# Embedding ranked over the rotary tables, a third more of expert 0 split ahead of the overflow check, and delta-rule key tiles of one chunk

## Chip, cores and metric

One core of one Trainium2 chip. The metric is the device time of one execution in microseconds, here the median over runs. Engines are called TensorE (PE), VectorE (DVE), ScalarE (ACT), GpSimd (POOL) and SyncE (SP, which issues most DMAs); L and a number is a line of the kernel.

## What is computed

An encoder trunk of two layers over 16 learned tokens and 1024 input tokens of width 1024, in float32. Shortened from the reference:

```python
h = layer_norm(concat([meta, x]), emb_ln_g, emb_ln_b)
cos, sin = rotary(pos)                        # used by the attention's latents
for li in range(2):
    proj = h @ w_in[li]
    y_att  = mla(c_q, c_kv, k_pe, cos, sin, ...)      # latent attention, 4 heads
    y_rwkv = rwkv_bidir(shifted(rw), ...)             # delta rule, 8 heads of 64, forward + backward
    h = layer_norm(a * h + concat([y_att, y_rwkv]) @ w_out[li])
    h = layer_norm(a * h + hier_moe(h))               # 32 experts, top-2 of one group
return h[:, 16:]

# the delta rule, per head and direction
S = S * w_t - (S @ kk_t) b_t' + v_t k_t' ;  y_t = S @ r_t
```

## The kernel before

Each layer runs in stages: input projection, attention, delta rule, output projection with the router, MoE. A scheduler orders most of the program from the code's order, priorities and its own estimate of times; the MoE's main loop stands in a `manual_schedule()` block and keeps the order in which it is written.

**Start (L279 to L291, L391 to L398).** `embed` takes the 16 learned tokens and then eight tiles of 128 tokens: a load `xt` on SP, a sum on ScalarE (L288), the layer norm on VectorE with a power on GpSimd (L223 to L228), a store to `h_rows`, and a transpose into `hT`, whose high and low parts (`hT_hi`, `hT_lo`) feed the input projection (L201 to L203). Ahead of it in the code stand the rotary tables (L240 to L265; tiles `pi`, `pf`, `ki`, `kf`, `trig`) and per-layer parameters (`cp`, `dcp`).

**MoE (`moe_layer`).** The weights of an expert come as three thirds of 1 MB (`raw`). `third` splits each into a high part on ScalarE (`w_hi`, L1217, four pieces) and a low part on VectorE (`w_lo`, L1221, four pieces). Before the main loop two thirds of expert 0 are split, and a branch (L1309) leads to code for tokens over an expert's capacity; the branch isn't taken at run time here. Then gathered tokens are transposed (`turned`), multiplied with the first two thirds (`first`), gated, transposed again (`upright`), and multiplied with the last third (`product`). `portion(e, q)` splits third q of expert e at its place in the loop. A load of weights needs a free `raw` tile, so it waits on SP for the split of an earlier third.

**Delta rule (`rwkv`, L1488 on).** The sequence is 17 chunks of 64, and two directions walk them, so there are 34 chunk steps a layer, in 17 jobs of two steps (one forward, one backward). A job passes four stages: `grams` (L1495) loads key tiles `T` and `BK`, multiplies them (`e`, L1528), masks the result into T and `AA`, scales BK and transposes it into `BT` (`m`, L1547); `blocks` and `levels` invert the triangular blocks (L1597 to L1618); `chain` (L1638) runs the recurrence, reading T at L1659 (`tu`) and L1666 (`y`), BT at L1683 (`st`), AA at L1690 (`y`), with a state tile `ring` that new_ring (L1625 on) fills on SP. The chains go one behind the other; grams run some jobs ahead. The output projection of the attention (`e` at L201 to L203, with stores and loads `a_d`, `ht`, `yraw` on SP) is filled in between.

T, AA and BT belong to a pool pair that alternates every second job (`svs[j % 4 // 2]`, each with two buffers), so the T of a job takes the buffer of the job four before. BK has two buffers of its own:

```python
T = sv[0].tile([128, U, 2, 128], F32, name="T")        # U = 8: both chunks of the job
BK = kb.tile([128, U, 2, 64], F32, name="BK")
BT = sv[1].tile([128, U, 2, 64], F32, name="BT")
```

Of the kernel before, what the change touches and what calls it, by code (L numbers as in the profile page):

```python
# [11 lines left out]
F32 = mybir.dt.float32  # L12
# [158 lines left out]
def hybrid_encoder(ctx: ExitStack, tc: tile.TileContext, I, out):  # L171
# [184 lines left out]
    for li in range(DEPTH):  # L356
# [32 lines left out]
        with pool(tc, name="ip", bufs=1, side="right") as ip, pool(tc, name="ipw", bufs=2, side="right") as wp, \  # L389
# [2 lines left out]
                pool(tc, name="ipp", bufs=2, space=PSUM) as pp, ExitStack() as late:  # L392
            hT = pair(ip, [128, 8, L], "hT")
            if li == 0:
                embed(hT, pp)
            else:
                combine(li - 1, hT, pp)
            wk = late.enter_context(pool(tc, name="ipk", bufs=1))  # L398
# [781 lines left out]
def moe_layer(tc, I, li, last, K, split, mm3, stack, rt, route, h1_rows, y_rows, nt, dram):  # L1180
# [18 lines left out]
    with pool(tc, name="mop", bufs=1, space=PSUM) as pp:  # L1199
# [177 lines left out]
        nb, nbi, known = excess()  # L1377

        with tc.issue_after(route.act.ins), tc.issue_after(route.dve.ins), tc.issue_after(known.ins), tc.issue_after(second.ins):
            ws = {0: [third(raws[0][q]) for q in range(2)]}  # L1380
        overflow(nb, nbi)


# [24 lines left out]
        with tc.manual_schedule():  # L1408
            xTs[0] = turned(xs[0], CAP)
            first(0, 0)  # L1410
            tokens(2)
            first(0, 1)
            tanh(0)
            gate(0)
            xTs[1] = turned(xs[1], CAP)
            tokens(3)
            portion(0, 2)
            raws.append(of(2))
            aT = upright(ths.pop(0), CAP)
            for q in range(3):  # L1420
                portion(1, q)
            raws.append(of(3))
            for e in range(NE):
                more, new = e + 1 < NE, e + 2 < NE
                if more:
                    first(e + 1, 0)
                portion(e + 2, 0)
                if new:

                    xTs[e + 2] = turned(xs[e % 2], CAP)  # L1430
                    if e + 4 < NE:
                        tokens(e + 4)
                if more:
                    first(e + 1, 1)
                if new:
                    mid, w1 = raws[e + 2][1], pair(ww, [128, 2048], "w")
                    ws[e + 2].append(w1)
                    for c in range(4):
                        high(mid, w1, c)
                        if c < 3:  # L1440
                            low(mid, w1, c)
                if more:
                    tanh(e + 1)
                    gate(e + 1)
                py = product(aT, ws.pop(e)[2], CAP)
                y = wk.tile([128, D], F32, name="y")
                if new:
                    low(mid, w1, 3)
                    raw, w = raws[e + 2][2], pair(ww, [128, 2048], "w")
                    ws[e + 2].append(w)  # L1450
                    for c in range(2):
                        high(raw, w, c)
                        low(raw, w, c)
                scaled(y, py, e, 0)
                if more:
                    aT = upright(ths.pop(e + 1), CAP)
                scaled(y, py, e, 1)
                nc.gpsimd.indirect_dma_start(out=views[e], out_offset=bass.IndirectOffsetOnAxis(ap=VS[:CAP, e:e + 1], axis=0),  # L1458
                                             in_=y[:CAP], in_offset=None, bounds_check=2 * n_rows - 1, oob_is_err=False)
                if new:  # L1460
                    for c in range(2, 4):
                        high(raw, w, c)
                        low(raw, w, c)
                    if e + 4 < NE:
                        raws.append(of(e + 4))


def rwkv(tc, li, last, K, P, pc, kr_d, bk_d, bon_d, g_dram, vt_d, yT, mhalf, kept, side, ready):
# [29 lines left out]
    def grams(runs, sv):  # L1498
# [1 line left out]

        U = 4 * sum(n for _, _, n in runs)

        T = sv[0].tile([128, U, 2, 128], F32, name="T")
        BK = kb.tile([128, U, 2, 64], F32, name="BK")

        at, u0 = [], 0
        for d, c0, n in runs:
            us = slice(u0, u0 + 4 * n)
            at += [(d, c0 + u // 4, u % 4) for u in range(4 * n)]
            u0 += 4 * n  # L1510
            for o, h in enumerate(HALF):
                nc.sync.dma_start(T[h, us, o], kr_d[d, h, c0:c0 + n].rearrange("p c i x -> p (c i) x"))
            cs = bk_d[d, :, c0:c0 + n].rearrange("p c i (a t) -> p (c i) a t", a=2)
            nc.sync.dma_start(BK[lo, us], cs[lo])
            for a in range(2):

                nc.sync.dma_start(BK[hi, us, 1 - a], cs[hi, :, a])
        AA = sv[1].tile([128, U, 128], F32, name="AA")
        A, AR = AA[:, :, :64], AA[:, :, 64:]
        BT = sv[1].tile([128, U, 2, 64], F32, name="BT")  # L1520


        for q0 in range(0, U, 4):
            q = slice(q0, q0 + 4)
            ps = [pe.tile([128, 4, 128], F32, name="e") for _ in HALF]
            for u in range(4):
                for o, h in enumerate(HALF):
                    nc.tensor.matmul(ps[o][:, u], BK[h, q0 + u].rearrange("p a t -> p (a t)"), T[h, q0 + u, o],  # L1528
                                     start=True, stop=True)
            mask = K(f"mask{at[q0][0]}")  # L1530
            for o in range(2):
                a, b = HALF[o], HALF[1 - o]
                V.tensor_tensor(T[b, q, o], ps[o][b], mask[b, None, :].to_broadcast([64, 4, 128]), op=OP.mult)  # L1533
                nc.scalar.activation(AA[a, q], ps[o][a], AF.Copy)  # L1534
        u0 = 0
        for d, c0, n in runs:
# [7 lines left out]
        for q0 in range(0, U, 4):  # L1544
            ps = bank().rearrange("p (a b) -> p a b", a=4)
            for u in range(4):
                nc.tensor.transpose(ps[:, u], BK[:, q0 + u].rearrange("p a t -> p (a t)"), ident)  # L1547
            nc.scalar.activation(BT[:, q0:q0 + 4].rearrange("p u o x -> p u (o x)"), ps, AF.Copy)
        return T, A, AR, BT, {x: u for u, x in enumerate(at)}

    def blocks(As, E):
# [84 lines left out]
    shared = {}  # L1636

    def chain(job, s, Y):  # L1638
        T, _, AR, BT, units = s
        for d, c in job:  # L1640
            ring = rings.pop((d, c))
            x = steps.index((d, c))
            if x + AHEAD < len(steps):
# [12 lines left out]
            tu, ps = shared["tu"][:, x % 2], shared["st"][:, x % 2]  # L1656
            for i in range(4):
                for o in range(2):
                    nc.tensor.matmul(tu[HALF[o], i], T[:, un(i), o, 0:64], ring[:, i, o], start=True, stop=True)  # L1659
            t0 = ch.tile([128, 4, 64], F32, name="t0", bufs=2)  # L1660
            nc.scalar.activation(t0, tu, AF.Copy)
            if want:
                py = pq.tile([128, 4, 64], F32, name="y", bufs=2)
                for i in range(4):
                    for o in range(2):
                        nc.tensor.matmul(py[HALF[o], i], T[:, un(i), o, 64:], ring[:, i, o], start=i == 0, stop=False,  # L1666
                                         skip_group_check=True)
            if more:
                nring = rings[d, orders[d][pos + 1]]
# [10 lines left out]
            if more:  # L1680
                for i in range(4):
                    for o in range(2):
                        nc.tensor.matmul(ps[HALF[o], i], BT[:, un(i), o], ring[:, i, o], start=True, stop=True)  # L1683
                for o in range(2):
                    a = HALF[o]
                    V.tensor_tensor(nring[a, :, o], ps[a], sp[a], op=OP.add)  # L1686
# [108 lines left out]
```

## Time and profile before

| | us |
|---|---|
| median of three runs (lowest, highest) | 3145.37 (3142.09, 3153.57) |
| the profiled execution | 3157.96 |
| its span | 3156.2 |
| TensorE busy in it | 2707.3 (86%) |
| VectorE busy | 2165.3 (69%) |
| ScalarE busy | 1650.5 (52%) |
| GpSimd busy | 1050.7 (33%) |
| mean granted TensorE clock | 0.888 |

The profile is one execution. Busy time of TensorE is the time in which matmuls are under way, at whichever clock was granted; 1.00 is 2.4 GHz and 0.50 is 1.2 GHz. A matmul of the program in plain float32 stands as two records in the trace. Idle time is named after what ended it. The stages lie, in us, at: layer 0 start and input projection 0 to 385, attention to 660, delta rule to 1120, output projection and router to 1200, MoE to 1545; layer 1 the same, with the delta rule at 2250 to 2700 and the MoE at 2760 to 3100.

### The profile page before, as it was taken

What the parts mean: (1) busy time and instruction counts of PE and PEld (TensorE: products, weight loads), DVE (VectorE), ACT (ScalarE), POOL (GpSimd) and SP (SyncE); (2) the same over time, 40 slices, a digit from 0 to 9 for tenths busy, and PEclk for the clock granted to TensorE, in tenths of its full rate; (3) what the DMA queues carried; (4) which work ended last, traced back from release to release, by engine and by line L of the source; (5) the groups of instructions that cost most, each with busy time, mean ns of one, the idle gap of its engine ahead of it and who ended that gap; (6) DMA issues with size and microseconds to landing.
All of it is one profiled execution on the core that took longest, in us unless ns stands there. A gap on an engine that the chain in (4) does not pass through costs nothing. (4 is left out here: it accounts for less than half of the span.)

```text
span 3156.2 us, 58039 instructions
## 1 busy us (share of the span) xinstructions
PE 2707.3 (86%) x22160; PEld 2209.1 (70%) x22160; DVE 2165.3 (69%) x4257; ACT 1650.5 (52%) x3604; POOL 1050.7 (33%) x1049
## 2 busy tenths in 40 slices
PE   5998799979999997999589997988799989799982
PEld 4888688768777775666388866877687777666661
DVE  7568655475766678989756756444667675789896
ACT  5434454444444447888543435434544453488882
POOL 3656211143334532121246631111433353321111
PEclk9999999978887897999789988998788879899996
DMA  5345610233322357999824465201433233699996
GB/s 175 97 137 185 205 48 21 75 93 102 94 68 78 108 198 259 358 360 352 303 91 137 155 194 186 65 21 51 107 108 101 69 93 100 214 333 356 352 347 244
DMA packets 342732, 523.77 MB, mean 166 GB/s; under 512 B 110732, under 2 KB 263308, under 8 KB 315808
## 3 DMA queue, kind: packets, MB, share of 16 engines
q1 hardware_dynamic: 234832, 399.11, 38.8%
q10 hardware_dynamic: 93280, 87.04, 8.1%
q0 software_dynamic: 14336, 33.84, 3.2%
q8 instruction: 176, 2.88, 0.4%
q14 instruction: 108, 0.88, 0.1%
HBM read 406.57 MB, written 129.84 MB: 170 GB/s over the span
## 5 line engine op out<-in xcount | busy, mean ns | idle before, releaser
L1221 DVE TENSOR_TENSOR w_lo<-raw,w_hi 128x512 fp32r<-128x512 f32 x768 | 481.7, 684 | 49.4 <-ACT w_hi L1217 49.1
L1217 ACT ACTIVATE w_hi<-raw 128x512 fp32r<-128x512 f32 x768 | 424.7, 625 | 71.0 <-DMA raw<-in_w_moe_dram 57.3
L201 PE MATMUL pj<-hT_hi,w_hi 128*128 128x352 f32 (+1 forms) x912 | 303.9, 334 | 3.0 <-ACT k L437 2.7
L202 PE MATMUL pj<-hT_lo,w_hi 128*128 128x352 f32 (+1 forms) x912 | 301.8, 331 | 2.8 <-DVE hT_lo L212 2.8
L203 PE MATMUL pj<-hT_hi,w_lo 128*128 128x352 f32 (+1 forms) x912 | 300.3, 330 | 0.0
L201 PE MATMUL ph<-w_hi,xT_hi 128*96 128x512 f32 x512 | 213.8, 418 | 3.9 <-ACT w_hi L1217 3.9
L202 PE MATMUL ph<-w_lo,xT_hi 128*96 128x512 f32 x512 | 206.0, 402 | 1.4 <-DVE w_lo L1221 1.4
L1458 POOL DMA_INDIRECT y_rows<-y,VS x64 | 59.9, 936 | 440.1 <-ACT y L1405 440.1
L1528 PE MATMUL e<-T,BK 64*128 64x128 f32 x1072 | 181.0, 352 | 28.5 <-DMA T<-kr_d 19.0
L203 PE MATMUL ph<-w_hi,xT_lo 128*96 128x512 f32 x512 | 205.3, 401 | 0.0
L212 DVE TENSOR_TENSOR pT_lo<-tr,pT_hi 128x512 fp32r<-128x512 f32 (+2 forms) x176 | 101.3, 592 | 130.1 <-ACT pT_hi L209 129.7
L201 PEld LDWEIGHTS pj<-hT_hi,w_hi 128*128 128x128 f32 x912 | 177.2, 195 | 13.3 <-issue 7.5
L1528 PEld LDWEIGHTS e<-T,BK 64*128 64x128 f32 x1072 | 152.7, 244 | 44.9 <-DMA T<-kr_d 15.6
L202 PEld LDWEIGHTS pj<-hT_lo,w_hi 128*128 128x128 f32 x912 | 176.8, 194 | 9.3 <-issue 4.9
L203 PEld LDWEIGHTS pj<-hT_hi,w_lo 128*128 128x128 f32 x912 | 176.4, 194 | 4.9 <-issue 4.3
L1533 DVE TENSOR_TENSOR T<-e,cc 64x512 f32<-64x512 f32 x134 | 92.2, 688 | 103.8 <-PE e L1528 101.2
L1673 POOL TENSOR_TENSOR sp<-ring,pc 64x256 f32<-64x256 f32 x126 | 84.7, 672 | 171.6 <-DVE ring L1686 150.8
L209 ACT ACTIVATE pT_hi<-tr 128x512 fp32r<-128x512 f32 (+2 forms) x176 | 87.0, 517 | 99.9 <-PE tr L873 98.3
L1277 POOL DMA_INDIRECT xs<-h_rows,XS x64 | 77.3, 1208 | 159.9 <-PE tp L1235 97.0
L1570 DVE TENSOR_TENSOR sb<-sb,dg 128x16 f32<-128x16 f32 (+8 forms) x270 | 106.5, 395 | 32.0 <-POOL dg L1562 24.8
L1540 POOL TENSOR_TENSOR AA<-AA,cc 128x256 f32<-128x256 f32 x67 | 52.0, 777 | 221.4 <-ACT AA L1534 161.8
L421 POOL TENSOR_SCALAR w_hi<-w_raw 128x1024 fp32r<-128x1024 f32 x34 | 102.3, 3010 | 59.4 <-PE pj L202 59.4
(422 smaller groups left out, 7678.3 us busy)
## 6 DMA issues: line engine op xcount, KB each, us to landing
raw<-in_w_moe_dram SPq DMA_DIRECT2D x192, 1024.0 KB
w_raw<-in_w_in_dram SPq DMA_DIRECT2D x38, 512.0 KB
T<-kr_d SPq DMA_DIRECT2D x134, 128.0 KB
ys<-y_rows SPq DMA_DIRECT2D x16, 1024.0 KB
a_d<-ht SPq DMA_DIRECT2D x25, 512.0 KB
h_rows<-h ACTq DMA_DIRECT2D x24, 512.0 KB
kr_d<-KR ACTq DMA_DIRECT2D x16, 576.0 KB
bk_d<-BK ACTq DMA_DIRECT2D x16, 576.0 KB
```

Source lines behind the costliest of these rows:

```text
L201: nc.tensor.matmul(o, a.hi, b.hi, start=start, stop=False)
L202: nc.tensor.matmul(o, a.hi, b.lo, start=False, stop=False)
L203: nc.tensor.matmul(o, a.lo, b.hi, start=False, stop=stop)
L209: hi = nc.scalar.activation(dst.hi, src, AF.Copy)
L212: return hi, e_lo.tensor_tensor(dst.lo, src, dst.hi.bitcast(F32), op=OP.subtract)
L421: nc.gpsimd.tensor_scalar(w.hi, wr, 1.0, None, op0=OP.mult)
L1217: nc.scalar.activation(w.hi[:, cs], raw[:, cs], AF.Copy)
L1221: V.tensor_tensor(w.lo[:, cs], raw[:, cs], w.hi[:, cs].bitcast(F32), op=OP.subtract)
L1528: nc.tensor.matmul(ps[o][:, u], BK[h, q0 + u].rearrange("p a t -> p (a t)"), T[h, q0 + u, o], start=True, stop=True)
L1533: V.tensor_tensor(T[b, q, o], ps[o][b], mask[b, None, :].to_broadcast([64, 4, 128]), op=OP.mult)
L1570: V.tensor_tensor(sb[:, :, cs], sb[:, :, cs], dg[:, :, t_:t_ + 1].to_broadcast([128, n, w]), op=OP.mult)
L1673: nc.gpsimd.tensor_tensor(sp[a], ring[a, :, o], pc[a, d, :, c:c + 1].to_broadcast([64, 4, 64]), op=OP.mult)
```

## The change

1. `embed` is recorded under `tc.high_priority()`, so the scheduler ranks its instructions over those of the rotary tables and parameters.
2. Expert 0's last third is split with the other two, ahead of the overflow check, instead of inside the main loop.
3. In `grams`, T and BT become tiles of one chunk with four buffers each, in place of tiles of two chunks with two. Memory, loads and matmuls are the same; each chunk's tile is released by its own last reader. BK and AA stay tiles of a job.

```diff
@@ input projection
             if li == 0:
-                embed(hT, pp)
+                with tc.high_priority():
+                    embed(hT, pp)
@@ moe_layer
-            ws = {0: [third(raws[0][q]) for q in range(2)]}
+            ws = {0: [third(raws[0][q]) for q in range(3)]}
         overflow(nb, nbi)
...
             tokens(3)
-            portion(0, 2)
             raws.append(of(2))
@@ grams
-        T = sv[0].tile([128, U, 2, 128], F32, name="T")
+        T, BT = {}, {}
         BK = kb.tile([128, U, 2, 64], F32, name="BK")
...
-            for o, h in enumerate(HALF):
-                nc.sync.dma_start(T[h, us, o], kr_d[d, h, c0:c0 + n].rearrange("p c i x -> p (c i) x"))
+            for c in range(c0, c0 + n):
+
+                T[d, c] = sv[0].tile([128, 4, 2, 128], F32, name="T", bufs=4)
+                for o, h in enumerate(HALF):
+                    nc.sync.dma_start(T[d, c][h, :, o], kr_d[d, h, c])
...
-        BT = sv[1].tile([128, U, 2, 64], F32, name="BT")
...
+            bt = BT[at[q0][:2]] = sv[1].tile([128, 4, 2, 64], F32, name="BT", bufs=4)
-            nc.scalar.activation(BT[:, q0:q0 + 4].rearrange("p u o x -> p u (o x)"), ps, AF.Copy)
+            nc.scalar.activation(bt.rearrange("p u o x -> p u (o x)"), ps, AF.Copy)
@@ chain: the readers index the chunk's own tile
+            T, BT = Ts[d, c], BTs[d, c]
-                    nc.tensor.matmul(tu[HALF[o], i], T[:, un(i), o, 0:64], ring[:, i, o], start=True, stop=True)
+                    nc.tensor.matmul(tu[HALF[o], i], T[:, i, o, 0:64], ring[:, i, o], start=True, stop=True)
```

Lines after the first part are one higher in the changed kernel, and those after `grams` four or five higher.

SP in the delta rule of layer 0, one job before the change (T four loads, one for each half of each chunk):

```order
L1630 DMA ring<-vt_d 64x4x64 x2
L1512 DMA T<-kr_d 64x4x128 x4
L959 DMA yraw<-yatt_d 128x4x128
L963 DMA ht<-h_rows_103 128x1024
L1630 DMA ring<-vt_d 64x4x64 x2
L1514 DMA BK<-bk_d 64x512
L1517 DMA BK<-bk_d 64x4x64 x2
L1514 DMA BK<-bk_d 64x512
L1517 DMA BK<-bk_d 64x4x64 x2
L1630 DMA ring<-vt_d 64x4x64 x2
L1512 DMA T<-kr_d 64x4x128 x4
```

And one job now:

```order
L1634 DMA ring<-vt_d 64x4x64 x2
L1515 DMA T<-kr_d 64x4x128 x2
L972 DMA a_d<-ht 128x1024
L960 DMA yraw<-yatt_d 128x4x128
L964 DMA ht<-h_rows_103 128x1024
L1634 DMA ring<-vt_d 64x4x64 x2
L1515 DMA T<-kr_d 64x4x128 x2
L1517 DMA BK<-bk_d 64x512
L1520 DMA BK<-bk_d 64x4x64 x2
L1517 DMA BK<-bk_d 64x512
L1520 DMA BK<-bk_d 64x4x64 x2
L1634 DMA ring<-vt_d 64x4x64 x2
```

The four T loads in one place have become two and two: the second pair of a job stands behind one `ring` pair, and the first pair of the next job behind the following `ring` pair, ahead of the BK loads where it stood behind them.

TensorE in the delta rule of layer 0 before the change, at the two sets of transposes of a job's BK (`m`, L1547):

```order
L1528 MATMUL e<-T,BK 128x128
L1618 MATMUL m<-Y,W 32x32 x16
L1547 MATMUL m<-cc,BK 128x128 x4
L1528 MATMUL e<-T,BK 128x128 x7
L1677 MATMUL tu<-t_8958,Y 64x64
L1547 MATMUL m<-cc,BK 128x128 x4
L1677 MATMUL tu<-t_8958,Y 64x64 x7
```

Twelve matmuls of the output projection and more than a whole step of the chain follow before the grams (`e`) that read the next BK. A place like it now:

```order
L1682 MATMUL tu<-t_8980,Y 64x64
L1550 MATMUL m<-cc,BK 128x128 x4
L1682 MATMUL tu<-t_8980,Y 64x64 x7
L1688 MATMUL st<-ring,BT 64x64
L1695 MATMUL y<-ring,AA 64x64
L1688 MATMUL st<-ring,BT 64x64 x7
L1695 MATMUL y<-ring,AA 64x64 x7
L1664 MATMUL tu<-ring,T 64x64 x8
L1531 MATMUL e<-T,BK 128x128 x4
```

The second chunk's transposes (L1550) come within one chain step of the next job's grams; BK's loads wait for them.

VectorE at the start of the MoE main loop of layer 0 before:

```order
L212 TENSOR_TENSOR xT_lo<-tp,xT_hi 128x4x96 x2
L1401 SCALAR_TENSOR_TENSOR th<-th,ph 96x256
L1402 SCALAR_TENSOR_TENSOR th<-th,ph 96x256
L212 TENSOR_TENSOR xT_lo<-tp,xT_hi 128x4x96 x2
L1221 TENSOR_TENSOR w_lo<-raw,w_hi 128x512 x4
L212 TENSOR_TENSOR aT_lo<-tp,aT_hi 128x2x96
L1221 TENSOR_TENSOR w_lo<-raw,w_hi 128x512 x16
L212 TENSOR_TENSOR xT_lo<-tp,xT_hi 128x4x96 x2
```

And now, with the nine pieces of w_lo ahead of the branch in front:

```order
L1222 TENSOR_TENSOR w_lo<-raw,w_hi 128x512 x3
L212 TENSOR_TENSOR xT_lo<-tp,xT_hi 128x4x96 x2
L1402 SCALAR_TENSOR_TENSOR th<-th,ph 96x256
L1403 SCALAR_TENSOR_TENSOR th<-th,ph 96x256
L212 TENSOR_TENSOR xT_lo<-tp,xT_hi 128x4x96 x2
L212 TENSOR_TENSOR aT_lo<-tp,aT_hi 128x2x96
L1222 TENSOR_TENSOR w_lo<-raw,w_hi 128x512 x16
L212 TENSOR_TENSOR xT_lo<-tp,xT_hi 128x4x96 x2
```

Of the four pieces that stood between the token tile and `aT_lo` none is left there; one went ahead of the branch (eight stood there) and three behind it, at the head of the loop.

## Rows read from the trace of the kernel before

**Rows 1.** The windows view by stage: from and to in us, length, busy us of TensorE (records), of its weight loads, of VectorE, ScalarE and GpSimd, then the mean granted TensorE clock, the DMA share and GB/s. Delta rule of layer 0, MoE of layer 0, delta rule of layer 1.

```profile
660.00:1120.00 460.00, 416.55 (x5963) 343.69 (x5965) 304.32 (x795) 197.93 (x459) 186.03 (x198) 0.80 0.34 97
...
1200.00:1545.00 345.00, 306.45 (x1472) 213.98 (x1472) 295.41 (x539) 279.18 (x568) 66.00 (x63) 0.97 0.96 342
...
2250.00:2700.00 450.00, 404.98 (x5813) 336.78 (x5814) 296.59 (x791) 199.13 (x462) 182.21 (x191) 0.82 0.35 101
```

**Rows 2.** What TensorE waited for in the delta rule of layer 0 (660 to 1120 us): instruction, releaser, us in total, times, longest.

```profile
PE tu L1659 <- DMA ring<-vt_d: 10.4, 1, 10.4
PE e L1528 <- DMA T<-kr_d: 9.2, 7, 2.8
PE e L1528 <- ACT AA L1534: 6.6, 8, 1.9
```

**Rows 3.** The same for the delta rule of layer 1 (2250 to 2700 us).

```profile
PE tu L1659 <- DMA ring<-vt_d: 17.7, 1, 17.7
PE e L1528 <- DMA T<-kr_d: 9.7, 5, 2.2
```

**Rows 4.** The windows view around two of the waits for T, columns as in the first group: the 20 us ahead of the wait and the 20.5 us behind it, twice.

```profile
718.50:738.50 20.00, 19.01 (x314) 15.64 (x312) 14.75 (x42) 10.41 (x25) 7.69 (x9) 1.00 0.30 85
738.70:759.20 20.50, 20.50 (x189) 17.19 (x189) 14.66 (x37) 9.24 (x22) 5.85 (x7) 0.50 0.26 74
817.70:837.70 20.00, 17.41 (x332) 14.70 (x332) 12.35 (x40) 10.97 (x27) 8.98 (x11) 1.00 0.29 78
837.70:858.20 20.50, 20.47 (x190) 17.28 (x191) 11.95 (x34) 9.24 (x22) 4.47 (x5) 0.50 0.16 42
```

**Rows 5.** The windows view of the nine stretches of clock 0.50 that begin with a wait for T or within 4 us of one (from 738.70, 837.70, 892.30, 943.50, 970.80, 1001.50, 2414.60, 2469.20 and 2575.10 us): the line that adds them up, columns as above.

```profile
sum 143.50, PE 142.31 PEld 120.05 DVE 92.09 ACT 68.22 POOL 33.02; mean PE 15.81 PEld 13.34 DVE 10.23 ACT 7.58 POOL 3.67
```

**Rows 6.** The timeline of SP, 880 to 892 us: start, us that the issues took, instruction, count.

```profile
882.35 0.46 SPq L1514 DMA_DIRECT2D BK<-bk_d  x1
...
887.30 1.20 SPq L1630 DMA_DIRECT2D ring<-vt_d  x2
888.60 3.46 SPq L1512 DMA_DIRECT2D T<-kr_d  x4
```

**Rows 7.** The timeline of TensorE in the same stretch; in brackets the idle time before and what ended it.

```profile
881.34 0.98 PE L1547 MATMUL m<-cc,BK 128*128 128x128 f32 x4
...
884.68 0.33 PE L1683 MATMUL st<-ring,BT 128*64 128x64 f32 x2
...
887.03 1.15 PE L1602 MATMUL m<-Y,W 64*64 64x64 f32 x32
...
889.09 0.56 PE L1666 MATMUL y<-ring,T 128*64 128x64 f32 x10
892.47 0.79 PE L1528 MATMUL e<-T,BK 64*128 64x128 f32 x2 [2.82 <-DMA T<-kr_d]
```

**Rows 8.** The timeline of ScalarE at the start of the MoE of layer 0.

```profile
1204.88 1.13 ACT L209 ACTIVATE xT_hi<-tp 128x384 fp32r<-128x384 f32 x2 [6.64 <-PE tp L1235]
...
1214.34 2.19 ACT L1217 ACTIVATE w_hi<-raw 128x512 fp32r<-128x512 f32 x4
```

**Rows 9.** The timeline of VectorE there.

```profile
1205.40 1.20 DVE L212 TENSOR_TENSOR xT_lo<-tp,xT_hi 128x384 fp32r<-128x384 f32 x2 [3.77 <-ACT xT_hi L209]
...
1215.33 2.48 DVE L1221 TENSOR_TENSOR w_lo<-raw,w_hi 128x512 fp32r<-128x512 f32 x4
...
1218.00 1.88 DVE L1221 TENSOR_TENSOR w_lo<-raw,w_hi 128x512 fp32r<-128x512 f32 x3
```

**Rows 10.** The timeline of TensorE there.

```profile
1217.31 0.74 PE L201 MATMUL ph<-w_hi,xT_hi 128*96 128x512 f32 x1 [1.93 <-ACT w_hi L1217]
1218.74 0.74 PE L202 MATMUL ph<-w_lo,xT_hi 128*96 128x512 f32 x1 [0.68 <-DVE w_lo L1221]
```

**Rows 11.** The timeline of SP there, 1217 to 1219 us.

```profile
1217.84 0.33 SPq L1211 DMA_DIRECT2D raw<-in_w_moe_dram  x1
```

**Rows 12.** The windows view of six us there, columns as in the first group.

```profile
1212.00:1218.00 6.00, 2.89 (x17) 1.71 (x15) 4.35 (x9) 4.80 (x11) 0.96 (x1) 0.88 0.30 91
```

**Rows 13.** What engines waited for in 1280 to 1520 us, well inside the MoE of layer 0: the line on the landing of expert weights.

```profile
ACT w_hi L1217 <- DMA raw<-in_w_moe_dram: 25.0, 28, 2.0
```

**Rows 14.** The timeline of VectorE in the first 28 us; `pf` and `kf` belong to the rotary tables, `dcp` to parameters, `xt` and `ht` to the embedding.

```profile
12.56 1.22 DVE L254 SCALAR_TENSOR_TENSOR pf<-kf,pf 128x1040 f32<-128x1040 f32 x1
...
13.81 1.24 DVE L254 SCALAR_TENSOR_TENSOR pf<-kf,pf 128x1040 f32<-128x1040 f32 x1
...
16.29 0.68 DVE L257 TENSOR_SCALAR kf<-pf 128x1040 f32<-128x1040 f32 x1
...
19.35 2.31 DVE L366 TENSOR_TENSOR dcp<-cp 128x15 f32<-128x15 f32 x1
...
21.66 2.32 DVE L371 TENSOR_SCALAR dcp<-cp 128x4 f32<-128x4 f32 x1
...
24.05 1.22 DVE L258 SCALAR_TENSOR_TENSOR pf<-kf,pf 128x1040 f32<-128x1040 f32 x1
25.20 1.27 DVE L228 SCALAR_TENSOR_TENSOR ht<-xt,ln_st,eb 128x1024 f32<-128x1024 f32 x1
```

**Rows 15.** The timeline of GpSimd there.

```profile
18.61 5.35 POOL L422 TENSOR_TENSOR w_lo<-w_raw,w_hi 128x1024 fp32r<-128x1024 f32 x2
```

**Rows 16.** The timeline of TensorE there.

```profile
40.66 0.66 PE L201 MATMUL pj<-hT_hi,w_hi 128*128 128x352 f32 x1
```

More of the change, by code (lines that the diff above doesn't have):

```diff
@@ L1525, in grams @@
             ps = [pe.tile([128, 4, 128], F32, name="e") for _ in HALF]
+            Tq = T[at[q0][:2]]
             for u in range(4):
                 for o, h in enumerate(HALF):
-                    nc.tensor.matmul(ps[o][:, u], BK[h, q0 + u].rearrange("p a t -> p (a t)"), T[h, q0 + u, o],
+                    nc.tensor.matmul(ps[o][:, u], BK[h, q0 + u].rearrange("p a t -> p (a t)"), Tq[h, u, o],
                                      start=True, stop=True)
@@ L1532, in grams @@
                 a, b = HALF[o], HALF[1 - o]
-                V.tensor_tensor(T[b, q, o], ps[o][b], mask[b, None, :].to_broadcast([64, 4, 128]), op=OP.mult)
+                V.tensor_tensor(Tq[b, :, o], ps[o][b], mask[b, None, :].to_broadcast([64, 4, 128]), op=OP.mult)
                 nc.scalar.activation(AA[a, q], ps[o][a], AF.Copy)
@@ L1638, in chain @@
     def chain(job, s, Y):
-        T, _, AR, BT, units = s
+        Ts, _, AR, BTs, units = s
         for d, c in job:
+            T, BT = Ts[d, c], BTs[d, c]
             ring = rings.pop((d, c))
@@ L1665, in chain @@
                     for o in range(2):
-                        nc.tensor.matmul(py[HALF[o], i], T[:, un(i), o, 64:], ring[:, i, o], start=i == 0, stop=False,
+                        nc.tensor.matmul(py[HALF[o], i], T[:, i, o, 64:], ring[:, i, o], start=i == 0, stop=False,
                                          skip_group_check=True)
@@ L1682, in chain @@
                     for o in range(2):
-                        nc.tensor.matmul(ps[HALF[o], i], BT[:, un(i), o], ring[:, i, o], start=True, stop=True)
+                        nc.tensor.matmul(ps[HALF[o], i], BT[:, i, o], ring[:, i, o], start=True, stop=True)
                 for o in range(2):
```

## Prediction

> **What bounds the kernel now.** I read the stages first, then the waits of TensorE in the stage that the change touches most, then the clock around those waits, then the queue that feeds them.
>
> The two delta-rule stretches are 910 us of the span, with TensorE busy 416.55 of 460 us and 404.98 of 450 us at a mean granted clock of 0.80 and 0.82, against 0.97 in the MoE stretch [rows 1]. TensorE bounds them, and loses time in two ways: waits, and a low clock. Of the waits, the gram matmuls (`e`, L1528) stand for their key tile T 9.2 us in 7 waits in layer 0 and 9.7 us in 5 in layer 1; only the one wait for `ring` at the start of each stage is larger [rows 2, 3]. The reader is to see that these 18.9 us are the small part. In the 20 us ahead of two such waits TensorE starts 314 and 332 matmul records at clock 1.00; in the 20.5 us behind them 189 and 190 at 0.50, the 1.2 GHz level [rows 4]. That is 16.15 records per us against 9.24, so a low stretch loses 1 - 9.24/16.15 = 0.43 of its length. Nine such stretches begin at or just behind a T wait, six of them in layer 0; together 143.5 us [rows 5], or 0.43 x 143.5 = 61.7 us lost.
>
> Why T is late: SP issues in order. In the job at 881 us the transposes of BK (L1547) run at 881.34 and release the BK loads at 882.35; then come two `ring` loads at 887.30, then four T loads from 888.60, over 3.46 us, which wait for the last reader of the tile four jobs back [rows 6]. TensorE has nothing else and starts `e` at 892.47 after 2.82 us idle, 3.87 us behind the first T issue [rows 7]. So a load that is released less than some 3.9 us of TensorE work ahead of its gram makes TensorE wait.
>
> In the MoE stage ACT takes 2.19 us for the four pieces of w_hi of expert 0's last third at 1214.34, between the first and the second expert, when both engines are wanted [rows 8]; DVE's w_lo of it lasts 2.48 us from 1215.33, and expert 1's begins only at 1218.00 [rows 9], though both engines sat idle before the first token tile at 1205. TensorE waits 1.93 and 0.68 us there [rows 10]. The next load of weights leaves at 1217.84 [rows 11], and in 1212 to 1218 the DMA engines are busy 0.30 [rows 12]. Later the stage goes by landings: ACT waits for them 28 times in 240 us [rows 13].
>
> At the start VectorE works on the rotary tables among the layer norms: tile 0's last step (L228) begins at 25.20 [rows 14], with GpSimd's w_lo splitting beside it [rows 15], and the first projection matmul is at 40.66 [rows 16].
>
> **The change, part by part.** It adds and removes no instruction of weight: the same T loads of 128 KB in the same number, the same splits, the same embedding. All is order and buffers.
>
> *Embedding first.* In the new order one L254, one L257 and one L258 stand behind tile 0's L228 that stood ahead: 1.22 + 0.68 + 1.22 = 3.1 us [rows 14]. Their results are wanted much later, by the rotary latents. I take 3 us off the first projection and off the end, since TensorE has no slack after it. Bounds: all table work between 12.56 and 25.20 gone from the chain is 1.22 + 1.24 + 0.68 + 2.31 + 2.32 + 1.22 = 9.0 us of gain [rows 14] the other way, one w_lo now stands ahead of tile 0's power on GpSimd, half of 5.35 = 2.7 us of loss [rows 15]. The value is nearest to the rows that really moved. SP's issues are permuted with the same bytes ahead of tile 0, so I cost that at nothing; were the consts late, the casts behind them would be late, not the layer norm.
>
> *Expert 0's third.* Four w_hi move to a time when ACT is idle and four w_lo likewise (one ahead of the branch, three behind); DVE has 3.77 us idle and ACT 6.64 us before the first token tile, more than the 2.48 and 2.19 that come [rows 8, 9]. Cover gone (if the gathers landed earlier), the loss would be those 2.5 us. Where they stood, VectorE's chain to expert 1's w_lo gets shorter by at most its 2.48 us. The load that left at 1217.84 [rows 11] can leave as soon as the third is split, some 11 us earlier, into the idle 0.70 x 6 = 4.2 us of the DMA engines [rows 12]; since the stage goes by landings, that is the upper bound. The lower is zero. I take VectorE's 2.5 us, which lies between and is the row nearest to what expert 1 waits for, twice, as layer 1 runs the same code: 5 us, bounds 0 to 8.4.
>
> *Key tiles by chunk.* T of a job's first chunk needs only the tile freed one chain step earlier. I counted in both orders, for the 13 steady jobs of each layer, the TensorE work between what a load must wait for and the gram that reads it, at 0.049 us a record (48 records from 884.68 to 887.03 [rows 7]; a matmul of the chain is two records) and a quarter us for one of the output projection. Before, the first chunk's T has 3.6 us or less in 15 of 26 jobs, and 12 waited. Now it has 10 us or more in all of them: the T waits go. But BK is still one tile per job, and its release moved the other way. With BT per chunk the second chunk's transposes (L1550) stand later, in front of the step that reads them, and BK's loads wait for both chunks' transposes. Its margin was 6.3 us or more; now it is 2.8 us in six jobs and 3.4 to 3.9 in three or four. Three BK issues and a landing take at least T's 3.9 us. So something like 8 places are tight where 15 were: by the same ratio 12 x 8/15 = 6.4 waits, I say 7 stay and 5 go. The second chunk's T keeps 5.5 us or more, enough.
>
> A wait costs 18.9/12 + 61.7/12 = 6.7 us. Five fewer: 34 us. Bounds: all twelve gone, 80.6 us; as many as before, 0; more than before is the last rival. I take the value by the count, not the middle.
>
> On the clock: the rows show a drop behind nine of twelve T waits, and full clock up to them. The Trainium skill, page "TensorE: Matmul & The Clock Gate", section "A second HAM failure mode: psum-queue depth-cycling", says against this that many short idles between groups of matmuls, with no transfer to blame, are enough to make the clock swing. By the rows the five waits bring back 5 x 5.1 = 26 us of clock; by that rule alone 0, since the short waits for ACT and DVE stay [rows 2]. I go by the rows: full clock up to the wait, half clock for the 20.5 us behind it [rows 4].
>
> Sum: 3 + 5 + 34 = 42 us. The profiled execution took 3157.96 us, so the sum gives 3116 for it; it was 12.6 us above the median of the three runs, and I put the same 42 us on the median: 3145.4 - 42 = **3103 us**.
>
> **The rivals.** *The clock stays.* Another short wait (AA 6.6 us in 8 [rows 2]) takes the clock down where T did. For: a mean clock of 0.80 over 460 us is 184 us at half clock, and the nine stretches of both layers hold only 143.5 [rows 1, 5]. Against: the clean edges in [rows 4]. Then five waits return 5 x 1.58 = 8 us only: 3145 - 8 - 8 = 3129 us.
>
> *BK takes T's place everywhere.* The narrow places all wait, the wider ones too when TensorE is quick because nothing stopped it before: still 12 waits. For: SP's BK loads stand behind `a_d`, which waits for VectorE, and behind two ring loads. Against: half of the jobs have 6 us or more. Then only the other two parts count: 3137 us.
>
> *Slower: BK waits in most jobs.* Place: the BK loads in SP's queue, behind the later transposes, with T and the last BK halves now behind the second `ring` wait. Each wait 6.7 us as now. It decides from 16 of the 26 steady jobs on: (16 - 12) x 6.7 - 8 = 19 us slower. With 17 it is 3145 + 34 - 8 = 3171 us. For: new order shows the release moved by some 50 matmuls. Against: only nine or ten margins are below 4 us.
>
> That a part does nothing (embedding behind the weights' landing, the third behind the gathers) is inside the bounds above, 8 us in all.
>
> **How the numbers follow.** Forecast 0.58, clock stays 0.13, BK in T's place 0.18, slower 0.11. The forecast's own range is two waits fewer (3145 - 13 - 8 = 3124) to all twelve gone (3145 - 80.6 - 8 = 3056). To reach 8 in 10 I take in the two middle rivals and the few us by which runs differ: 3056 to 3145. Within 0.5%, 16 us, about what a measurement of this kernel can tell from no change, lie the BK rival and half of the clock rival: 0.24. Faster: 0.58 + 0.07 = 0.65. Slower 0.11.
>
> **What would show it.** Right: the wait of `e` for T is near zero in both delta stretches, replaced by waits of `e` for BK, about 7 of 1 to 2 us; their mean clock rises by about 0.03 each; the MoE has no w_hi between experts 0 and 1 and a load leaves near 1206 on the old clock; the first projection matmul is at 37 to 38 us. Wrong: T waits that stay, a mean clock at or below 0.80, or BK waits in more than 12 jobs.

## The result, and the profile after

The change takes 3128.93 us (median of 11 runs, 3118.20 to 3136.64), the kernel before in the same rounds 3145.07 (11 runs, 3128.31 to 3153.57): ratio 0.995, 95% interval 0.993 to 0.997. In later rounds (e12) it was 0.992 (0.9891 to 0.9949). It is some 16 us faster where 42 were forecast: 3129 lies in the range, but the gain is well under half of the forecast.

The profiled execution took 3135.11 us, its span is 3133.3 us, and the mean granted TensorE clock 0.896 (0.888 before). The page's first part:

```profile
PE 2662.7 (85%) x22160; PEld 2173.7 (69%) x22160; DVE 2162.9 (69%) x4257; ACT 1644.5 (52%) x3604; POOL 1053.3 (34%) x1049
```

The table cuts the span where the first matmul of each stage starts, and the MoE where its last `ph` matmul starts (us, worked out from the starts in the trace; *again* is the second profile of the same kernel, e12):

| | start | proj 0 | att 0 | delta 0 | out 0 | MoE 0 | proj 1 | att 1 | delta 1 | out 1 | MoE 1 | end |
|---|---|---|---|---|---|---|---|---|---|---|---|---|
| before | 40.7 | 333.1 | 254.8 | 493.8 | 83.0 | 327.4 | 412.6 | 266.0 | 484.8 | 66.0 | 326.8 | 67.0 |
| change | 38.6 | 352.4 | 261.0 | 461.4 | 88.1 | 325.9 | 408.1 | 259.5 | 471.6 | 71.4 | 326.2 | 69.1 |
| again | 38.5 | 355.2 | 260.3 | 461.0 | 85.1 | 325.3 | 410.6 | 260.0 | 470.2 | 71.6 | 324.3 | 68.9 |

Three things stand out: the delta rules are 32.4 and 13.2 us shorter, the first input projection is 19.3 us longer, and the MoE stages hardly move. (The attention of layer 0 took 257 to 265 us in every other profile, so 254.8 is a low value of before, not a loss. How far one profile can be off is seen in before and e14, whose matmuls stand in nearly the same order: delta rules of 493.8 and 484.8 us in one, 484.0 and 497.3 in the other.)

**Delta rule.** The windows view, columns as in [rows 1], of the two delta rules as the table cuts them, before:

```profile
628.63:1122.39 493.76, 446.01 (x6190) 369.00 (x6189) 329.49 (x861) 220.61 (x510) 199.07 (x210) 0.81 0.32 91
2211.52:2696.30 484.78, 426.65 (x5994) 356.11 (x5993) 321.52 (x869) 216.86 (x502) 196.60 (x207) 0.82 0.35 99
```

And in the change, with its MoE of layer 0 last:

```profile
652.02:1113.42 461.40, 410.82 (x6190) 340.67 (x6189) 326.16 (x861) 217.92 (x511) 198.78 (x209) 0.87 0.34 96
2195.05:2666.67 471.62, 404.80 (x5994) 336.76 (x5993) 323.57 (x871) 218.06 (x505) 195.83 (x207) 0.84 0.35 100
...
1200.00:1545.00 345.00, 304.12 (x1472) 212.34 (x1472) 292.31 (x534) 279.14 (x566) 69.38 (x64) 0.97 0.96 342
```

What TensorE waited for there, layer 0 (683 to 1111 us; total, times, longest):

```profile
PE tu L1664 <- DMA ring<-vt_d: 13.1, 1, 13.1
PE m L1615 <- DVE X L1608: 7.3, 5, 2.4
...
PE y L1671 <- DVE ring L1691: 5.2, 2, 4.7
PE e L1531 <- ACT AA L1537: 3.6, 5, 2.0
...
PE e L1531 <- DMA BK<-bk_d: 0.3, 1, 0.3
```

And layer 1 (2230 to 2670 us):

```profile
...
PE e L1531 <- ACT AA L1537: 9.3, 8, 2.8
PE y L1671 <- DVE yt L1698: 7.7, 3, 5.5
PE y L1671 <- DVE ring L1691: 6.0, 1, 6.0
...
PE e L1531 <- DMA BK<-bk_d: 0.4, 1, 0.4
```

The reader is to see what is missing: no line of `e` on T is left, where [rows 2, 3] have 18.9 us in 12 waits, and BK has two waits of 0.3 and 0.4 us. Other waits grew in their place: summed over the gaps of more than 0.2 us between the first chain matmul and the first matmul behind the stage (`po`, of the output projection), TensorE idles 84.3 us in the two layers, 75.1 before. But the clock rose, from 0.81 to 0.87 and from 0.82 to 0.84 (0.03 each was forecast): the stages hold the same 6190 and 5994 matmul records, and TensorE is busy with them for 57 us less. Added up from the clock in the traces, it stands at 1.2 GHz for 270 us of the two stages, before for 370. The other profiles agree: with T uncut (eight profiles) that time is 335 to 386 us and the two stages together last 973 to 999, with T cut (ten) 237 to 271 and 915 to 944.

**Start.** TensorE of the change:

```profile
38.58 0.66 PE L201 MATMUL pj<-hT_hi,w_hi 128*128 128x352 f32 x1
...
83.94 0.43 PE L201 MATMUL pj<-hT_hi,w_hi 128*128 128x352 f32 x1 [1.10 <-POOL w_hi L422]
...
88.17 0.65 PE L201 MATMUL pj<-hT_hi,w_hi 128*128 128x336 f32 x1 [3.32 <-ACT kk L438]
...
93.45 0.58 PE L491 MATMUL tp<-wd,wa_hi 128*128 128x288 f32 x1 [2.76 <-DVE wd L673]
```

GpSimd of the change, splitting the third and fourth weight blocks:

```profile
81.09 6.41 POOL L422 TENSOR_SCALAR w_hi<-w_raw 128x1024 fp32r<-128x1024 f32 x2 [1.77 <-PE pj L202]
87.48 2.36 POOL L423 TENSOR_TENSOR w_lo<-w_raw,w_hi 128x1024 fp32r<-128x1024 f32 x1
89.86 2.35 POOL L423 TENSOR_TENSOR w_lo<-w_raw,w_hi 128x1024 fp32r<-128x1024 f32 x1
```

And of the kernel before:

```profile
70.85 2.79 POOL L421 TENSOR_SCALAR w_hi<-w_raw 128x1024 fp32r<-128x1024 f32 x1 [3.54 <-PE pj L202]
73.72 3.17 POOL L422 TENSOR_TENSOR w_lo<-w_raw,w_hi 128x1024 fp32r<-128x1024 f32 x1
78.75 2.77 POOL L421 TENSOR_SCALAR w_hi<-w_raw 128x1024 fp32r<-128x1024 f32 x1 [1.79 <-PE pj L202]
```

The first projection matmul came 2.1 us earlier, where 3 were forecast. But the 181st, the first behind the blocks of weights that are there at the start, came at 99.5 us instead of 84.4, and that loss stays: the attention starts at 391.0 us instead of 373.8. Some of it is there at the 61st matmul, at 69.0 us instead of 65.4, since the later tiles of the embedding come later than before (GpSimd's last two powers at 56.3 and 61.2 us, before at 52.2 and 57.2); the larger part comes behind it. In TensorE's new order the transposes of the embedding's last tile stand among the matmuls of the second block, and the first block's last matmuls behind them. Weights have two buffers, so the split of the third block waits for the end of the first: 81.09 instead of 70.85. Both w_hi then come ahead of both w_lo, and the first w_lo is ready near 90 us instead of 77. The windows view of before and of the change, 50 to 100 us:

```profile
50.00:100.00 50.00, 46.68 (x279) 44.73 (x280) 27.74 (x27) 25.10 (x45) 23.29 (x29) 0.93 0.25 87
```

```profile
50.00:100.00 50.00, 36.69 (x195) 33.66 (x196) 25.53 (x28) 20.76 (x36) 19.35 (x27) 0.80 0.25 87
```

TensorE loses 10 us of work, and the clock falls too.

**MoE.** ScalarE, VectorE, and TensorE of the change, by timeline, and ScalarE's wait for landings in 1280 to 1520 us:

```profile
1190.36 6.33 ACT L1218 ACTIVATE w_hi<-raw 128x512 fp32r<-128x512 f32 x12
...
1211.70 8.42 ACT L1218 ACTIVATE w_hi<-raw 128x512 fp32r<-128x512 f32 x16
```

```profile
1193.11 7.54 DVE L1222 TENSOR_TENSOR w_lo<-raw,w_hi 128x512 fp32r<-128x512 f32 x12
```

```profile
1212.37 0.64 PE L201 MATMUL ph<-w_hi,xT_hi 128*96 128x512 f32 x1 [0.94 <-ACT w_hi L1218]
```

```profile
ACT w_hi L1218 <- DMA raw<-in_w_moe_dram: 25.1, 32, 1.5
```

All twelve pieces are split ahead of the first token tile, and TensorE's waits of 1.93 and 0.68 us at the second expert [rows 10] have become one of 0.94. A fourth load of weights leaves at 1202.5 us, 1206.3 on the clock of before, where it left at 1217.84 [rows 11]; near 1206 was forecast. Deeper in the stage the landings set the pace as before (25.0 us in [rows 13]).

### The profile page after: what moved, and what is told of

It is laid out like the page before. It is cut to its first block, busy times and chain, and to the rows that moved or that the text cites. A ratio compares the mean times of both kernels' runs of the same rounds, so it can differ in the third digit from the quotient of the medians.

```text
span 3133.3 us, 58061 instructions
## 1 busy us (share of the span) xinstructions
PE 2662.7 (85%) x22160; PEld 2173.7 (69%) x22160; DVE 2162.9 (69%) x4257; ACT 1644.5 (52%) x3604; POOL 1053.3 (34%) x1049
## 5 line engine op out<-in xcount | busy, mean ns | idle before, releaser
L1531 PE MATMUL e<-T,BK 64*128 64x128 f32 x1072 | 154.1, 327 | 15.3 <-ACT AA L1537 12.9
L1531 PEld LDWEIGHTS e<-T,BK 64*128 64x128 f32 x1072 | 128.9, 222 | 29.5 <-ACT AA L1537 16.2
L201 PE MATMUL o<-pT_hi,V_hi 128*128 128x256 f32 (+3 forms) x288 | 95.6, 332 | 28.0 <-ACT yatt L882 28.0
```

The costliest lines, as they stand in the source:

```text
L201: nc.tensor.matmul(o, a.hi, b.hi, start=start, stop=False)
```

## The experiments

Theory A at the outset: key tiles gain by the T waits and the clock behind them, and the ranked embedding costs what the key tiles gain more than the total. Rival B: the embedding is free, and the key tiles fell short. Each part alone, and the change without the embedding, on one chip (before: 3154.56 us).

**e1: the embedding alone.**

```diff
-                embed(hT, pp)
+                with tc.high_priority():
+                    embed(hT, pp)
```

> Only the embedding's rank is changed. Theory A (this part costs what the other two do not bring home): in the profile of the full change the third block of the projection starts 15 us later than before and the attention of layer 0 23 us later, so this kernel alone is 15 to 25 us slower than before (ratio 1.005 to 1.008), with the first projection matmul at about 38.6 us and the 181st near 99 us. Theory B (the rank is worth its 3 us, and the loss in layer 0 is the scheduler's reshuffling by the other parts): 0 to 3 us faster, 181st projection matmul near 82 us.

3187.47 us, ratio 1.0083 (1.0047 to 1.012). The first projection matmul is at 38.5 us, the 181st at 100.6. The embedding as ranked costs 26 us (15 to 38). In e1's profile the attention starts 18.6 us later than before, by the mechanism shown above; where the rest lies is not shown. The rank also moves what comes much later: lined up from the first chain matmul on, runs of like matmuls of TensorE taken as one row, e1's order differs from that of before in 710 of some 6950 rows.

**e2: the third alone.**

```diff
-            ws = {0: [third(raws[0][q]) for q in range(2)]}
+            ws = {0: [third(raws[0][q]) for q in range(3)]}
...
-            portion(0, 2)
```

> Only expert 0's last third is split ahead of the check. Theory A: 2.5 us are won per layer at expert 1 and one to two of them are given back where the stage goes by landings: 1 to 4 us faster (ratio about 0.999). Theory B (a load that leaves 11 us earlier is worth the idle DMA time): 5 to 8 us faster.

3156.64 us, ratio 0.9991 (0.9962 to 1.002): within the noise. The MoE stages are at 324.3 and 326.1 us; over the profiles up to e8 they average 326.8 and 327.6 without the edit and 325.6 and 325.7 with it, 3 us in both layers.

**e3: T and BT of one chunk alone** (the `grams` and `chain` parts of the diff).

> Only T and BT are cut to one chunk. Theory A: all T waits go and no BK wait comes, worth 32 us in layer 0 and 15 in layer 1 as in the full change: about 45 us faster (ratio 0.985 to 0.987), start and attention of layer 0 as before. Theory B (the gain in the delta rule is mostly the clock's chance in one profile): 20 us or less faster, ratio 0.993 or more.

3129.39 us, ratio 0.991 (0.9876 to 0.9944), 28 us (18 to 39). No wait for T is left. The gain is less than the 45 us of A and more than B's 20. The 46 us by which the two stages differ between the profiles of before and of the change overstate it: the profiled execution of before lies 12.6 us above its median, that of e3 some 4 below.

**e4: the change without the embedding's rank** (e2 and e3 together).

> The change without the embedding's rank. Theory A: keys and third together, 45 to 50 us faster than before (ratio 0.984 to 0.986), 30 us faster than the full change. Theory B: no faster than the full change, ratio 0.995.

3115.83 us, ratio 0.9861 (0.9825 to 0.9898). Without the rank the other two parts give 44 us by this run, 35 to 40 by its like (e10, e11 and e15, below). A holds by these ratios, on different chips: the rank takes back about half. On one chip it is less (e12, below).

Which part of the rank, and which of the tiles? On the next chip (before: 3158.25 us):

**e5: only the learned tokens and the first three token tiles ranked.**

```diff
-            for i, n, col in TILES[NT:] + TILES[:NT]:
+            for at, (i, n, col) in enumerate(TILES[NT:] + TILES[:NT]):
+                with tc.high_priority() if at < 4 else nullcontext():
```

> On the kernel before, only the learned tokens and the first three token tiles of the embedding get the higher rank; in the new order of TensorE the first projection block ends ahead of the second, as before the change. Theory A (the whole rank loses because the last tile's transposes are queued behind matmuls of the second block, so that the first block ends late, its weight buffers come free late and GpSimd splits the third block's weights 11 us late): the 181st projection matmul near 83 us instead of 100, time 0 to 4 us below the kernel before. Theory B (any reordering of the start that takes VectorE from the rotary tables loses later, because the tables are late): 10 us or more above the kernel before.

3159.19 us, ratio 1.0007 (0.998 to 1.0035). The first projection matmul is at 35.9 us, 4.8 us earlier than before, and the 61st at 65.0, where before has 65.4. So a gain of 4.8 us at the first matmul is 0.4 at the 61st: the later tiles set the pace, and 3 us there never were 3 us at the end.

**e6: e1 with the w_hi of the third and fourth block on ScalarE.**

```diff
-                early = len(projected) < 2
+                early = len(projected) < 4
```

> The whole embedding ranked high on the kernel before, and the high parts of the third and fourth projection blocks are made on ScalarE instead of GpSimd. Theory A: the release of the buffers stays at 81 us but the split behind it gets 5 us shorter, so the 181st projection matmul comes near 95 us instead of 100.6 and the time is some 5 us below the kernel that has the embedding's rank alone, still 10 to 20 us above the kernel before. Theory B (GpSimd's split is not on the path): unchanged, 26 us above the kernel before.

3151.23 us, ratio 0.998 (0.9953 to 1.0007). The 181st matmul is at 90.3 us. Taking one step out of GpSimd's late chain gives back 10 of 16 us at that place. The time misses both theories: A had it 10 to 20 us above before, and it is 6 below (15 below to 2 above). Some 20 us more came back than the start explains.

**e7: T of one chunk, BT of a job. e8: BT of one chunk, T of a job.**

```diff
-        T = sv[0].tile([128, U, 2, 128], F32, name="T")
+                T[d, c] = sv[0].tile([128, 4, 2, 128], F32, name="T", bufs=4)
```

```diff
-        BT = sv[1].tile([128, U, 2, 64], F32, name="BT")
+            bt = BT[at[q0][:2]] = sv[1].tile([128, 4, 2, 64], F32, name="BT", bufs=4)
```

> On the kernel before, T is cut to one chunk and BT stays a tile of two. Theory A (T's early issue is the whole gain, and BT by chunk only moves BK's release later): no wait of the grams for T, none for BK, 28 us or more below the kernel before, as with both cut. Theory B (the gain needs the transposes to move as well): half of it, 10 to 18 us.

> On the kernel before, BT is cut to one chunk and T stays a tile of two. Theory A: the grams wait for T some 12 times as before, the time is within 8 us of the kernel before. Theory B: 10 to 18 us faster.

e7: 3130.86 us, ratio 0.9908 (0.9881 to 0.9935). e8: 3162.78 us, 1.0009 (0.9984 to 1.0033). T alone carries the gain; BT neither gives nor takes. TensorE's waits of `e` in e7, layer 0 and then layer 1, have no T:

```profile
PE e L1532 <- ACT AA L1538: 9.3, 8, 3.8
```

```profile
PE e L1532 <- ACT AA L1538: 10.9, 8, 3.8
```

(One wait for BK, of 0.4 us, stands at 657 us, just ahead of the window of the first.) In e8 those for T stand as before:

```profile
PE e L1528 <- DMA T<-kr_d: 9.4, 7, 2.7
PE e L1528 <- ACT AA L1534: 6.6, 7, 1.9
```

```profile
PE e L1528 <- DMA T<-kr_d: 10.9, 6, 3.3
```

Then what the parts give together (before: 3158.97 us):

**e9: the change with e6's edit. e10: e7 with the third. e11: the change with the rank of e5. e12: the change again.**

> The full change, with the high parts of the third and fourth projection blocks made on ScalarE. Theory A (the embedding's rank loses through GpSimd's late and longer split of the third block's weights): the 181st projection matmul near 90 us as with the rank alone, 10 us of the start come back, time about 10 us below the full change (ratio to before about 0.991). Theory B (what the full change loses against the version without the rank lies in the delta rule's order): as the full change, 0.995.

> T by chunk and the third ahead, BT of two chunks, the embedding as before. Theory A (T alone carries the gain): 28 to 44 us below before, ratio 0.986 to 0.991, no T waits. Theory B (the third adds as much as the pair of runs with and without it suggested): nearer to 0.986.

> Keys and third of the change, and the higher rank for the learned tokens and the first three token tiles only. Theory A (the first matmuls 5 us earlier are worth nothing, since the later tiles set the pace): as without any rank, ratio 0.984 to 0.988, 181st projection matmul near 84 us. Theory B: 3 to 5 us better than that.

> The full change once more beside the others, on the same chip. Theory A: 10 us above the version with ScalarE's splits and 25 to 30 us above those without the whole rank, ratio to before 0.993 to 0.997. Theory B: within 5 us of the version with ScalarE's splits.

e9: 3102.27 us, ratio 0.9823 (0.9794 to 0.9852), the fastest version. e10: 3118.86, 0.9873 (0.9845 to 0.9901). e11: 3118.24, 0.9878 (0.9845 to 0.9911). e12: 3132.19, 0.992 (0.9891 to 0.9949). e10 and e11 say that neither BT nor the first tiles' rank add anything. e12 is 13 and 14 us above them, where A had 25 to 30: beside its like on one chip, the rank costs the change about half of what it costs alone. e9 is 30 us below the change where A had put some 10: its first projection is 10 us shorter than e12's, as A has it, but its delta rules are 7 and 9 us shorter too (454.5 and 460.9 us).

Two questions were left: does ranking the embedding cost in itself, or only through the order of the first blocks; and is ScalarE's splitting worth something without the rank? (Before: 3159.46 us.)

**e13: all nine tiles ranked, but not the loads of the layer norm's two rows** (`eg`, `eb`), which leaves the first blocks' matmuls in the order of before. **e16: the change with that rank.**

```diff
             g = bcast_row(wk, I["emb_ln_g"], D, "eg", bufs=1)
             b = bcast_row(wk, I["emb_ln_b"], D, "eb", bufs=1)
             for i, n, col in TILES[NT:] + TILES[:NT]:
+                with tc.high_priority():
...
```

**e14: before with e6's edit. e15: e4 with e6's edit.**

> The kernel before with all nine tiles of the embedding ranked, but not the two loads of its layer-norm rows (eg, eb). In this order the first block's matmuls are not split by the last tile's transposes. Theory A (the loss of the ranked embedding is the late end of the first block, not the ranking): the 181st projection matmul within 1 us of the 84.4 us of before, attention starts within 5 us of before, ratio 0.995 to 1.002. Theory B (ranking the embedding over the tables costs in itself, because the tables end later): the 181st matmul or the attention start later by 10 us or more, ratio 1.004 to 1.010.

> The kernel before with only the w_hi of the third and fourth weight block on ScalarE in place of GpSimd. Theory A (that edit only mends what the ranked embedding broke): the 181st projection matmul stays at 84 to 88 us, ratio 0.997 to 1.003. Theory B (the edit is worth something by itself, and made the earlier version with all parts fast): ratio 0.985 to 0.994.

> Key tiles of one chunk and the third, no ranked embedding, w_hi of the third and fourth block on ScalarE. Theory A (that edit mends only the ranked embedding): the ratio of the version without it, 0.983 to 0.990. Theory B (the edit is worth some 12 us by itself): 0.977 to 0.983.

> The whole change with the rank on the nine tiles alone, not on the loads eg and eb. Theory A (the loss was the late end of the first block): the 181st projection matmul within 1 us of 84.4, ratio 0.983 to 0.989, 10 to 25 us below the change as made. Theory B (ranking costs in itself): 0.990 to 0.995, as the change.

e13: 3153.29 us, ratio 0.9963 (0.9937 to 0.9989). e14: 3161.03, 0.9988 (0.9962 to 1.0014). e15: 3123.33, 0.9888 (0.9865 to 0.9911). e16: 3122.71, 0.989 (0.9868 to 0.9912). TensorE's first projection matmul in e13, and GpSimd's split of the third block:

```profile
36.27 0.66 PE L201 MATMUL pj<-hT_hi,w_hi 128*128 128x352 f32 x1
```

```profile
71.15 2.79 POOL L422 TENSOR_SCALAR w_hi<-w_raw 128x1024 fp32r<-128x1024 f32 x1 [3.55 <-PE pj L202]
74.02 3.17 POOL L423 TENSOR_TENSOR w_lo<-w_raw,w_hi 128x1024 fp32r<-128x1024 f32 x1
```

The same nine tiles are ranked and the split is back at 71 us, the 61st matmul at 65.7 and the 181st at 84.7, and the loss is gone: it lay in the order that came with the two loads' rank, not in ranking the tiles. The late tiles and the late end of the first block went together, so their shares are not told apart. (e13's order also leaves no wait of `e` for T over 0.2 us in the delta rule of layer 0, with T uncut, and TensorE is at 1.2 GHz there for 133 us, where the seven other versions with T uncut have 156 to 194; in layer 1 it has seven such waits and 202 us. It is one profile, but here too the clock goes with the waits.) e16 places the 181st matmul at 83.6 us and is 9 us faster than e12, a little less than the 10 to 25 expected; the two ran on different chips and their intervals meet.

e14 and e15 show that ScalarE's splitting is worth nothing without the rank. That does not settle the 20 us beyond the start that e6 and e9 gained. Lined up as above, the edit moves 4 and 5 rows of TensorE's order in e14 (against before) and e15 (against e4), but 377 and 438 in e6 (against e1) and e9 (against the change); two profiles of one kernel differ in none. So under the rank it also reshuffles what comes later, and no run separates the two. By the trace e9's stages differ from e12's by 3 to 10 us in several places, and its time at 1.2 GHz over the whole span is 604 us, against 644. Which waits do it stays open.

## Why the prediction was wrong, point by point

**Embedding: the step that failed.** "3 us off the first projection and off the end, since TensorE has no slack after it" took the first matmul for the pace of the stage. The 2.1 us there are real; e5 shows 4.8 us there shrink to 0.4 by the 61st matmul. And "all is order and buffers" was followed for VectorE and GpSimd only: the working never asked which weight buffer the new order of TensorE frees late. That costs 26 us alone (e1); in the whole change 18 us is the estimate, from 0.9935, the mean of its two ratios, against 0.9878, the mean of e4, e10, e11, e15 and e16; the start alone is 17.2 us longer in its profile, and on one chip the difference is 13 to 14 us. The bounds, -9.0 to +2.7, did not hold it. This is about 21 of the 26 us that are missing.

**Third: the mechanism was right, the size too large.** w_hi and w_lo moved under idle engines, and TensorE's two waits of 2.61 us became 0.94. But of VectorE's 2.5 us a layer about 1.5 remain at the stage's end, since the landings take the rest back. That is 3 us, not 5, by stage lengths; the time of e2 (12 us faster to 6 slower) can't tell the two apart.

**Key tiles: right in sum, by two errors that cancel.** Five of twelve waits were to go; all twelve went. The seven BK waits did not come. SP and then TensorE in the change at one of the five tightest places:

```profile
2414.67 0.47 SPq L1517 DMA_DIRECT2D BK<-bk_d  x1
...
2416.68 1.48 SPq L1520 DMA_DIRECT2D BK<-bk_d  x2
```

```profile
2413.99 0.66 PE L1550 MATMUL m<-cc,BK 128*128 128x128 f32 x4
...
2415.78 0.33 PE L1688 MATMUL st<-ring,BT 128*64 128x64 f32 x2 [0.53 <-ACT ring L1683]
...
2418.12 1.16 PE L1531 MATMUL e<-T,BK 64*128 64x128 f32 x8
```

Two things were wrong here. Counting records at 0.049 us left out what TensorE itself stands still for in between: some 60 records are 2.9 us by the count, but from the end of the transposes (2414.65) to the first `e` there are 3.47 us, 0.53 of it a wait for ScalarE's `ring`; the five places have 3.41 to 3.47. And the load needs less than the 3.9 us of "three BK issues and a landing": the first `e` starts 3.45 us behind the first BK issue, when the third is only just issued, and does not wait. A gram's first matmul reads only the half that the first of a chunk's three loads brings. The two waits for BK that did come (0.28 and 0.36 us) stand at later matmuls of a gram, one at such a place and one where the count would have given 4.5 us.

The price was wrong the other way. Twelve waits at 6.7 us would be 80.6; e3 and e7 measured 28 and 29, or 2.4 us each. Idle time did not fall, since AA, X, `ring` and `yt` came late instead; only time at 1.2 GHz did, 370 to 270 us. At 0.43 of its length, as the prediction priced it, that is 43 us, and 34 with the 9 us more of idle time taken off: near to e3 and e7, within what single profiles allow.

**The sum** by what the runs showed: -18 + 3 + 28 = 13 us, against the measured 16 (9 to 22, from the interval).

**The rivals.** "The clock stays" named 3129 us and the time is 3129, but not by its mechanism: it had five T waits go without any gain of clock, and the clock is what was gained; that it named the time is luck. Its half truth is that other short waits take the clock down as well (last section). The Trainium skill, page "TensorE: Matmul & The Clock Gate", section "A second HAM failure mode: psum-queue depth-cycling", tells of a kernel whose frequent short idles between groups of matmuls make the clock swing; by that rule alone the key tiles' gain of clock was 0. The traces disagree: with 9 us more of idle time, 100 us less at 1.2 GHz. "BK takes T's place everywhere" and "Slower" are refuted by 0.7 us of BK waits in all. None of the rivals had the embedding in it: its harm was bounded, not imagined.

## What to carry to other kernels

Where a scheduler orders the program, an edit at the start is to be priced by the last consumer that it displaces, not by the first that it helps: look in the new order of the bounding engine for a group of matmuls that now ends later, and ask which buffer it frees. A wait that is taken away returns its idle time only if nothing else is late behind it, so price that at zero first, and the clock behind it from windows around waits that will take its place. And test a rank on part of its instructions: two loads less under it made a loss of 26 us disappear.

## What the runs showed of the hardware that was not expected

Waits of one length differ in what they cost in clock. For every wait of TensorE in the delta rules of all 18 profiles with a mean clock of at least 0.95 in the 6 us ahead of it, I worked out the time at 1.2 GHz in the 24 us behind: waits of 1 to 2 us of `e` for a key tile's load 15.3 us (37 waits, all for T), of `e` for AA 7.3 us (35), all other waits of 1 to 2 us 6.9 us (125). Nor do waits over 4 us cost more than those for T: 11.2 us (27). The 37 stand in the eight profiles with T uncut, at much the same places of the schedule, so they are fewer cases than their number says. Two cases by the windows view, columns as in [rows 1]. In e8, ahead of and behind a wait of 1.64 us for T:

```profile
879.10:899.10 20.00, 19.01 (x362) 15.92 (x358) 9.89 (x22) 10.98 (x27) 8.84 (x11) 1.00 0.34 89
900.80:917.80 17.00, 17.00 (x185) 14.47 (x185) 11.29 (x38) 8.38 (x20) 2.12 (x3) 0.54 0.08 21
```

In the change, ahead of and behind a wait of 6.04 us for VectorE's `ring`:

```profile
2426.30:2446.30 20.00, 18.93 (x355) 15.78 (x354) 16.02 (x56) 10.11 (x26) 7.88 (x10) 1.00 0.34 92
2452.40:2472.40 20.00, 19.37 (x293) 16.67 (x294) 7.99 (x13) 10.46 (x25) 8.91 (x11) 0.77 0.19 57
```

The wait a quarter as long has the lower clock behind it (0.57 over 20 us, against 0.77). Why is not shown; it may lie in the work that stands around a gram, which no run here varied.
